# A hybrid transformer block on one core: four groups of w_down by seven products, a ring of four places, a new order of jobs

## The chip, the core and the metric

The kernel runs on one core of a Trainium2 chip. TensorE (PE) multiplies matrices, VectorE (DVE) and ScalarE (ACT) work on elements, GpSimd (POOL) here starts only DMAs that add to what they find, SyncE (SP) starts the other DMAs. The metric is the device time of one execution in microseconds (us); the profile is one further execution of the same program.

## What is computed

Two layers over x of 512 tokens by 1024 columns. Each layer norms x, projects it, runs three mixers side by side (a gated linear recurrence, a differential attention, a second recurrence), adds their projection to x, and ends in an MLP with a squared relu. The MLP is all that the change touches:

```
for l in range(DEPTH):                       # 2 layers
    ...                                      # mixers; x = x + mix @ w_out[l]
    h2 = rmsnorm(x, norm2_g[l])
    a = jnp.square(jax.nn.relu(h2 @ w_up[l]))      # 1024 -> 4096
    x = x + a @ w_down[l]                          # 4096 -> 1024
```

## The kernel before

A factor of a matrix product stands as two parts, a rounded high one (hi) and the rest (lo), and a product takes three matmuls, hi by hi, hi by lo and lo by hi. A weight **panel** of 512 KB is loaded, then made into `whi` and `wlo` in two halves: for each half ACT casts the raw data to `whi` (`halves`, L245) and DVE subtracts that from the raw data for `wlo` (L246). `whi` and `wlo` have three buffers each, so the casts of the panel of job n can start when the matmuls of job n-3 are done.

The 4096 columns between w_up and w_down are cut into 8 **groups** of 512, and the work on them into jobs, each of one panel:

- a **u** is one of seven products by which w_up of the next group is computed (`up_group`; seven products of quarter blocks in place of eight). In the order of the jobs they are p5, p1, p2, p7, p6, p4, p3; each has 24 matmuls of 128x256 (L1147 to L1149, in `product`). The results meet in `tmp` on DVE: after p6 three adds read the banks of p7 and p5 (L1183 to L1186), and p3 ends in L1197. `put` then takes relu and square on ACT and splits the result into hi and lo (`split`: cast L1090, subtraction L1091).
- a **d** is a quarter of an ordinary w_down group (`down_group`): 24 matmuls of 128x512 (L297 to L299), added to x by DVE (L1004).
- an **s** is one of seven products of a w_down group that is listed in `SEVEN`, here groups 2, 4 and 6 (`down_seven`): 12 matmuls of 128x512. It needs sums of quarter blocks of the squares (the **forms**), which DVE makes and `split` stores in the places `S["ah"][0]` and `S["al"][0]`, and its results go to x or to four accumulators (L1233, L1235, L1237), which `add_up` adds to x behind the last such group (L1258, L1262, L1267).

Some panels are sums of blocks of weights. They stand in four raw buffers (`raw(0)` to `raw(3)`, halves of the tiles mA and kT): SP loads a first block (`block_panel`, L262), and POOL starts a DMA that adds the next one to it (L264). The same buffer is then used by a later product: DMAs of POOL add a further block to it, once the halves of the product before have been read. So there are **chains**: in a u group p7 adds to what p1 used, p6 to what p5 used, and p3 to what p6 used. Panels that are no sums come through a ring of two buffers, `wraw`.

What sets the order is the table `ORDER`: string g gives the jobs of row g, which are the w_down of group g and the w_up of group g+1. The program is written out job by job, and the panel of job n+2 is begun ahead of job n (`AHEAD = 2`). Each engine then runs its instructions in its own order and waits for what is not yet there. In PSUM the results of p5, p7 and p3 share two banks (`ax`), p1 and p6 have one (`hx`), p2 and p4 one (`pv`), and the d and s jobs four (`mm`).

Of the kernel before, what the change touches and what calls it, by code (L numbers as in the profile page):

```python
# [15 lines left out]
P = 128  # L16
# [13 lines left out]
WP = 1056  # L30
WARM = 2
TOP = 1 << 24
SEVEN = (2, 4, 6)
ORDER = ("duduuduuduu", "uuduudududu", "usuusuusuus", "ususududusudud", "usuusuusuus", "ususududusudud", "usuusuusuus",
         "sssdddd")
RB = 3
COLS = dict(mq=0, mk=256, mv=512, mo=768, aq=1032, ak=1544, av=2056, hq=2568, hf=2824, hi=3080)

# [26 lines left out]
def hybrid_kernel(ctx, tc, x, norm1_g, w_in, conv_w, gate_b, mlstm_g, qn_g, kn_g, lam_v, subln_g,  # L65
# [16 lines left out]
    V = nc.vector  # L82
# [672 lines left out]
    steps = []  # L755

    def add_layer(l):
# [370 lines left out]
        def up_group(g):  # L1130


            c0 = g * 512
            w = {(i, j): w_up[l, (j - 1) * 512:j * 512, c0 + (i - 1) * 256:c0 + i * 256]
                 for i in (1, 2) for j in (1, 2)}
            st = {}
            tmp = [slab(13 + n // 2, 512, off=512 * (n % 2)) for n in range(4)]

            def product(wt, name, tag):
                pt = ps(tag)  # L1140
                wh, wl = wt
                hh, hl = S["F"][name]
                for c in range(2):
                    col = slice(c * P, (c + 1) * P)
                    dst = pt[:, c * 256:(c + 1) * 256]
                    for k in range(4):
                        mm(dst, wh[:, k, col], hh[:, k], start=k == 0, stop=False)  # L1147
                        mm(dst, wh[:, k, col], hl[:, k], start=False, stop=False)  # L1148
                        mm(dst, wl[:, k, col], hh[:, k], start=False, stop=k == 3)  # L1149
                return pt  # L1150

            def put(src, i, j):

                n = 2 * i + j
                tok = slice(j * 256, (j + 1) * 256)

                def two(v):
                    return v.rearrange("p (c t) -> p c t", c=2)
                r = slab(0, 512, off=512 * (n % 2))
                act(r, src, AF.Relu)  # L1160
                if g in SEVEN:
                    act(a4()[:, n], r, AF.Square)
                    if n in (0, 2):
                        split(*place(n // 2), a4()[:, n])
                else:
                    act(r, r, AF.Square)
                    split(S["ah"][1][:, 2 * i:2 * i + 2, tok], S["al"][1][:, 2 * i:2 * i + 2, tok], two(r))

            def p1(wt):
                nc.scalar.copy(tmp[0], product(wt, "b11", "hx"))  # L1170

            def p5(wt):
                st["5"] = product(wt, "t1", "ax")

            def p2(wt):
                V.tensor_add(tmp[3], product(wt, "b21", "pv"), tmp[0])
                put(tmp[3], 0, 0)

            def p7(wt):
                st["7"] = product(wt, "t3", "ax")  # L1180

            def p6(wt):
                V.tensor_sub(tmp[1], product(wt, "t2", "hx"), tmp[0])  # L1183
                V.tensor_add(tmp[2], st["7"], tmp[1])
                V.tensor_sub(tmp[0], tmp[2], st["5"])
                V.tensor_sub(tmp[3], st["5"], tmp[1])  # L1186
                put(tmp[0], 1, 1)

            def p4(wt):
                if g == 4 and l + 1 < DEPTH:  # L1190
                    load_gains(l + 1)
                    prms[l + 1] = load_params(l + 1)()
                V.tensor_add(tmp[2], product(wt, "t4", "pv"), tmp[2])
                put(tmp[2], 1, 0)

            def p3(wt):
                V.tensor_add(tmp[3], product(wt, "b22", "ax"), tmp[3])  # L1197
                put(tmp[3], 0, 1)
                if g in SEVEN:
                    a = a4()  # L1200
                    V.tensor_sub(a[:, 0], a[:, 0], a[:, 1])
                    split(*place(2), a[:, 0])
                    V.tensor_sub(a[:, 1], a[:, 1], a[:, 3])
                    split(*place(3), a[:, 1])

            one, two_ = (0, 1) if g % 2 else (1, 0)
            return [((lambda: block_panel(raw(two_), w[2, 1], [w[2, 2]])), p5),
                    ((lambda: block_panel(raw(one), w[1, 1], [])), p1),
                    ((lambda: block_panel(in_ring(), w[1, 2], [])), p2),
                    ((lambda: block_panel(raw(one), None, [w[2, 1]])), p7),  # L1210
                    ((lambda: block_panel(raw(two_), None, [w[1, 1]])), p6),
                    ((lambda: block_panel(in_ring(), w[2, 2], [])), p4),
                    ((lambda: block_panel(raw(two_), None, [w[1, 2]])), p3)]

        def down_seven(g):

            w = {(i, j): w_down[l, g * 512 + (j - 1) * 256:g * 512 + j * 256, (i - 1) * 512:i * 512]
                 for i in (1, 2) for j in (1, 2)}  # L1220

            def product(wt, n, to, after=None):
                hi, lo = (t.rearrange("p (k t) -> p k t", k=2) for t in place(n))
                for c in range(2):
                    pt = ps("mm")
                    tok = slice(c * P, (c + 1) * P)
                    nat_mm(pt, 512, lambda k: hi[:, k, tok], lambda k: lo[:, k, tok], *wt,
                           [(0, 0), (1, 1)], True, True)
                    with tc.high_priority():
                        if isinstance(to, tuple):  # L1230
                            i, j = to
                            d = xs[2 * j + c][:, i * 512:(i + 1) * 512]
                            V.tensor_add(d, d, pt)  # L1233
                        elif g == SEVEN[0]:
                            nc.scalar.copy(acc(to)[:, c], pt)  # L1235
                        else:
                            V.tensor_add(acc(to)[:, c], acc(to)[:, c], pt)  # L1237
                if after:
                    after()

            def t2():
                a = a4()
                V.tensor_add(a[:, 0], a[:, 0], a[:, 3])
                split(*place(0), a[:, 0])

            def t4():
                a = a4()
                V.tensor_sub(a[:, 0], a[:, 2], a[:, 0])
                split(*place(1), a[:, 0])

            def b22():
                split(*place(2), a4()[:, 3])

            def add_up():
                def to_x(i, j, op, n):
                    for c in range(2):
                        d = xs[2 * j + c][:, i * 512:(i + 1) * 512]
                        op(d, d, acc(n)[:, c])  # L1258

                def s0():  # L1260
                    to_x(0, 0, V.tensor_add, 0)
                    V.tensor_sub(acc(2), acc(2), acc(0))  # L1262
                    to_x(0, 1, V.tensor_add, 1)
                    to_x(0, 1, V.tensor_sub, 2)

                def s1():
                    V.tensor_add(acc(3), acc(3), acc(2))  # L1267
                    to_x(1, 0, V.tensor_add, 3)
                    to_x(1, 1, V.tensor_add, 3)
                    to_x(1, 1, V.tensor_sub, 1)  # L1270
                if g == SEVEN[-1]:
                    steps.extend([s0, s1])

            def pan(r, fresh, add):
                return lambda: block_panel(r(), fresh, add, 512)
            one, two = (lambda: raw(2)), (lambda: raw(3))
            return [(pan(one, w[1, 1], []), None, None, lambda t: product(t, 0, 0)),
                    (pan(in_ring, w[1, 2], []), None, None, lambda t: product(t, 1, (0, 0), t2)),
                    (pan(two, w[2, 1], [w[2, 2]]), None, None, lambda t: product(t, 2, 1, t4)),
                    (pan(one, None, [w[2, 1]]), None, None, lambda t: product(t, 3, 3, b22)),  # L1280
                    (pan(two, None, [w[1, 1]]), None, None, lambda t: product(t, 0, 2)),
                    (pan(in_ring, w[2, 2], []), None, None, lambda t: product(t, 1, (1, 0))),
                    (pan(two, None, [w[1, 2]]), None, None, lambda t: product(t, 2, (0, 1), add_up))]

        def down_group(g):
            def st(i):
                return tuple((lambda k, t=t[g % 2]: t[:, k, i * P:(i + 1) * P]) for t in (S["ah"], S["al"]))

            def done(i, cols):
                if g < NG - 1:  # L1290
# [75 lines left out]
```

## Time and profile before

| | |
|---|---|
| median of 3 runs | 1270.45 us (1269.99 to 1270.73) |
| the profiled execution, device time | 1270.51 us |
| its span | 1268.7 us |
| PE busy | 1255.0 us, 99% |
| DVE busy | 987.2 us, 78% |
| ACT busy | 748.4 us, 59% |
| POOL busy | 120.5 us, 9% |
| MLP rows 0 to 7, layer 0 | 326.7 to 641 us |
| MLP rows 0 to 7, layer 1 | 956 to 1268 us |

Times inside the profile count from the start of the span; some 1.8 us of the execution lie outside it. A busy engine is one that has an instruction under way, and matmuls overlap, so the distance from start to start says what a matmul costs, not the time of one. The granted clock (PEclk, 1.00 is full) is TensorE's alone.

### The profile page before, as it was taken

The numbers are of one execution on the slowest core, as the hardware profiler recorded it, in microseconds if no ns is written. First come the engines' busy times: TensorE is split into PE (matmuls) and PEld (weight loads), VectorE is DVE, ScalarE is ACT, GpSimd is POOL, SyncE is SP. The second block draws the span as 40 slices with busy tenths as digits, with TensorE's granted clock in tenths as the row PEclk, the third lists the DMA queues.
The fourth block names the chain that finished last, engine by engine and source line by source line (L and its number), as shares of the span: only waits on it lengthen the run. The fifth ranks groups of instructions, "written<-read, shape, count | busy, mean of one in ns | idle before, by whom it ended". The sixth has DMA issues, their size and how long they took to land.

```text
span 1268.7 us, 20162 instructions
## 1 busy us (share of the span) xinstructions
PE 1255.0 (99%) x7420; PEld 1076.1 (85%) x7420; DVE 987.2 (78%) x2190; ACT 748.4 (59%) x1607; POOL 120.5 (9%) x116
## 2 busy tenths in 40 slices
PE   9999999999999999999999999999999999999998
PEld 6788777888999988989787887788888989899896
DVE  6786887988966868779967767879888677677787
ACT  6754785638644745545556457756386547456461
POOL 0000000000011211211000000000001112121210
PEclk9999999999999999999999999999999999999999
DMA  7322211216576987877433222112265779878863
GB/s 212 84 67 70 66 34 51 83 55 170 130 166 133 197 188 164 183 183 134 116 83 83 68 74 61 34 50 83 64 170 117 167 143 198 195 155 203 171 123 110
DMA packets 116758, 153.43 MB, mean 121 GB/s; under 512 B 5738, under 2 KB 80052, under 8 KB 116660
## 3 DMA queue, kind: packets, MB, share of 16 engines
q1 hardware_dynamic: 80228, 109.66, 27.9%
q0 software_dynamic: 36096, 41.95, 21.6%
q8 instruction: 58, 0.95, 0.3%
q10 hardware_dynamic: 336, 0.54, 0.1%
q14 instruction: 40, 0.33, 0.1%
HBM read 150.03 MB, written 2.10 MB: 120 GB/s over the span
## 4 chain that ended last, share of the span: by engine, by line
PE 83%; DVE 6%; ACT 5%; DMA 3%; issue 1%; SPq 0%; POOL 0%; ACTq 0%; DVEq 0%; POOLq 0%
PE pmm L299 14%; PE pmm L297 14%; PE pmm L298 14%; PE pmm L305 3%; PE pmm L306 3%; PE pmm L304 3%; PE pax L1148 3%; PE pax L1147 3%; PE pax L1149 3%; PE pax L687 2%; PE phx L1148 2%; PE phx L1149 2%; PE phx L1147 2%; PE ppv L1147 2%; PE ppv L1148 2%; PE ppv L1149 2%
## 5 line engine op out<-in xcount | busy, mean ns | idle before, releaser
L297 PE MATMUL pmm<-whi,h 128*128 128x512 f32 (+2 forms) x484 | 187.3, 387 | 0.1
L298 PE MATMUL pmm<-wlo,h 128*128 128x512 f32 (+2 forms) x484 | 185.5, 384 | 0.2 <-DVE wlo L246 0.2
L245 ACT CAST whi<-wraw 128x512 fp32r<-128x512 f32 x192 | 109.4, 618 | 123.9 <-PE pmm L299 64.1
L299 PE MATMUL pmm<-whi,h 128*128 128x512 f32 (+2 forms) x452 | 173.3, 383 | 0.1
L246 DVE TENSOR_TENSOR wlo<-wraw,whi 128x512 fp32r<-128x512 f32 x192 | 125.7, 687 | 45.5 <-ACT whi L245 45.4
L288 ACT ACTIVATE whi<-wraw,gcol 128x256 fp32r<-128x256 f32 (+2 forms) x192 | 99.5, 572 | 80.3 <-PE pmm L299 63.9
L289 DVE SCALAR_TENSOR_TENSOR wlo<-wraw,gcol,whi 128x256 fp32r<-128x256 f32 (+2 forms) x192 | 101.8, 569 | 43.2 <-ACT whi L288 40.8
L298 PEld LDWEIGHTS pmm<-wlo,h 128*128 128x128 f32 x484 | 91.1, 188 | 16.9 <-DVE wlo L246 1.0
L297 PEld LDWEIGHTS pmm<-whi,h 128*128 128x128 f32 x484 | 91.1, 188 | 16.1 <-ACT h L343 0.5
L297 PE MATMUL pmm<-whi,yb 128*128 128x512 f32 (+2 forms) x256 | 100.4, 392 | 0.0
L299 PEld LDWEIGHTS pmm<-whi,h 128*128 128x128 f32 x452 | 85.0, 188 | 16.2 <-DVE h L1091 0.6
L298 PE MATMUL pmm<-wlo,yb 128*128 128x512 f32 (+2 forms) x256 | 98.5, 385 | 0.0
L245 ACT CAST whi<-kT 128x512 fp32r<-128x512 f32 x108 | 61.6, 618 | 52.5 <-DMA kT<-in_w_up_dram 14.1
L298 PE MATMUL pmm<-wlo,ya 128*128 128x512 f32 (+2 forms) x228 | 87.3, 383 | 0.0
L297 PE MATMUL pmm<-whi,ya 128*128 128x512 f32 (+2 forms) x228 | 87.3, 383 | 0.0
L299 PE MATMUL pmm<-whi,yd 128*128 128x512 f32 (+2 forms) x224 | 86.3, 385 | 0.3 <-DVE yd L1091 0.3
L246 DVE TENSOR_TENSOR wlo<-kT,whi 128x512 fp32r<-128x512 f32 x108 | 69.6, 685 | 19.0 <-ACT whi L245 18.4
L1004 DVE TENSOR_TENSOR x<-x,pmm 128x512 f32<-128x512 f32 x96 | 65.5, 683 | 22.4 <-PE pmm L299 21.4
L245 ACT CAST whi<-mA 128x512 fp32r<-128x512 f32 x92 | 52.4, 617 | 48.9 <-PE pmm L299 21.5
L299 PE MATMUL pmm<-whi,yc 128*128 128x512 f32 (+2 forms) x212 | 80.9, 381 | 0.0
L264 POOL DMA_DIRECT2D kT<-in_w_up_dram x30 | 38.9, 1298 | 409.9 <-DVE wlo L246 248.2
L246 DVE TENSOR_TENSOR wlo<-mA,whi 128x512 fp32r<-128x512 f32 x92 | 59.3, 685 | 13.6 <-ACT whi L245 13.6
(479 smaller groups left out, 3526.9 us busy)
## 6 DMA issues: line engine op xcount, KB each, us to landing
wraw<-in_w_down_dram SPq DMA_DIRECT2D x52, 512.0 KB
wraw<-in_w_in_dram SPq DMA_DIRECT2D x51, 512.0 KB
wraw<-in_w_up_dram SPq DMA_DIRECT2D x36, 512.0 KB
kT<-in_w_up_dram POOLq DMA_DIRECT2D x30, 512.0 KB, 6.5
mA<-in_w_up_dram POOLq DMA_DIRECT2D x26, 512.0 KB, 6.8
kT<-in_w_down_dram POOLq DMA_DIRECT2D x18, 512.0 KB, 7.3
wraw<-in_w_out_dram SPq DMA_DIRECT2D x16, 512.0 KB
mA<-in_w_up_dram SPq DMA_DIRECT2D x14, 512.0 KB
```

Of the source, the lines that this page charges most:

```text
L245: nc.scalar.copy(hi[:, ch], raw[:, ch])
L246: V.tensor_sub(lo[:, ch], raw[:, ch], hi[:, ch].bitcast(F32))
L264: nc.gpsimd.dma_start(out=v3(raw), in_=rows(b), accum_op=ALU.add)
L288: act(hi[:, ch], raw[:, ch], AF.Copy, scale=g)
L289: V.scalar_tensor_tensor(lo[:, ch], raw[:, ch], g, hi[:, ch].bitcast(F32), op0=ALU.mult, op1=ALU.subtract)
L297: mm(pt[:, :n], sh(a), wh[:, b], start=first and j == 0, stop=False)
L298: mm(pt[:, :n], sh(a), wl[:, b], start=False, stop=False)
L299: mm(pt[:, :n], sl(a), wh[:, b], start=False, stop=last and j == nk - 1)
L1004: V.tensor_add(xs[i][:, cols], xs[i][:, cols], pt)
L1147: mm(dst, wh[:, k, col], hh[:, k], start=k == 0, stop=False)
L1148: mm(dst, wh[:, k, col], hl[:, k], start=False, stop=False)
L1149: mm(dst, wl[:, k, col], hh[:, k], start=False, stop=k == 3)
```

## The change

Groups 2, 3, 4 and 5 are computed by seven products, not 2, 4 and 6. So two such groups follow each other, and the forms of group g+1 take places that products of group g still read: a small table says what each form needs (`needs`), `happened` is called behind each square and each product, and makes each form as soon as all it needs has happened, in a ring of four places. `BUF` says in which of the two buffers an ordinary group's squares stand: group 1 in buffer 1 as before, from which its jobs now run as late as row 4, group 6 in buffer 1 and group 7 in buffer 0. `add_up` follows group 5. `ORDER` is rewritten.

```diff
-SEVEN = (2, 4, 6)
-ORDER = ("duduuduuduu", "uuduudududu", "usuusuusuus", "ususududusudud", "usuusuusuus", "ususududusudud", "usuusuusuus",
-         "sssdddd")
+SEVEN = (2, 3, 4, 5)
+ORDER = ("duduuduuduu", "uuuuuuu", "susususdudsususu", "sususususususu", "susususdudsususu", "suusuusuusu",
+         "sususuduuduudd", "dddd")
...
+        BUF = {g: g % 2 for g in range(NG)}
+        BUF.update({NG - 2: 1, NG - 1: 0})
...
+        def form(g, k):
+            a = a4()
+            if k == 2:
+                V.tensor_sub(a[:, 0], a[:, 0], a[:, 1])
+            elif k == 3:
+                V.tensor_sub(a[:, 1], a[:, 1], a[:, 3])
+            elif k == 4:
+                V.tensor_add(a[:, 0], a[:, 0], a[:, 3])
+            elif k == 5:
+                V.tensor_sub(a[:, 0], a[:, 2], a[:, 0])
+            split(*place(k % 4), a[:, (0, 2, 0, 1, 0, 0, 3)[k]])
...
+        def happened(*what):
+            kind, g, n = what
...
+            seen.add(what)
+            for f in [f for f in forms]:
+                if needs(*f) <= seen:
+                    form(*f)
+                    forms.remove(f)
+                    seen.add(("form",) + f)
...
                 if g in SEVEN:
                     act(a4()[:, n], r, AF.Square)
-                    if n in (0, 2):
-                        split(*place(n // 2), a4()[:, n])
+                    happened("put", g, n)
                 else:
                     act(r, r, AF.Square)
-                    split(S["ah"][1][:, 2 * i:2 * i + 2, tok], S["al"][1][:, 2 * i:2 * i + 2, tok], two(r))
+                    ah, al = S["ah"][BUF[g]], S["al"][BUF[g]]
+                    split(ah[:, 2 * i:2 * i + 2, tok], al[:, 2 * i:2 * i + 2, tok], two(r))
...
-            def product(wt, n, to, after=None):
-                hi, lo = (t.rearrange("p (k t) -> p k t", k=2) for t in place(n))
+            def product(wt, n, to):
+                assert ("form", g, n) in seen
+                hi, lo = (t.rearrange("p (k t) -> p k t", k=2) for t in place(n % 4))
...
+                happened("product", g, n)
+                if n == 6 and g == SEVEN[-1]:
+                    add_up()
...
-                return tuple((lambda k, t=t[g % 2]: t[:, k, i * P:(i + 1) * P]) for t in (S["ah"], S["al"]))
+                return tuple((lambda k, t=t[BUF[g]]: t[:, k, i * P:(i + 1) * P]) for t in (S["ah"], S["al"]))
```

What this moves on the engines is seen in row 1, where the products of w_up of group 2 stand. The lines of the changed kernel have other numbers: L1176 is L1219 there, L1183 to L1186 are L1226 to L1229, L1160 is L1203, L1162 and L1166 are L1205 and L1208, L1170 is L1213.

DVE in layer 0, before, from the panel of p4 to that of p3. In a row the line stands first, then the operation, and what is written and read; wlo_587 is the low half of p4's panel, wlo_591 that of the fourth quarter of group 1, wlo_597 that of p3; phx_588 is the bank of p6's result, pax_581 that of p7, pax_564 that of p5:

```order
L246 TENSOR_TENSOR wlo_587_4020<-wraw_585_4018,whi_586_4019 128x512 x2
L1183 TENSOR_TENSOR big_67<-phx_588_4026,big_67 128x512
L246 TENSOR_TENSOR wlo_591_4059<-wraw_589_4057,whi_590_4058 128x512 x2
L1184 TENSOR_TENSOR big_67<-pax_581_3957,big_67 128x512
L1185 TENSOR_TENSOR big_67<-big_67,pax_564_3818 128x512
L1186 TENSOR_TENSOR big_67<-pax_564_3818,big_67 128x512
L246 TENSOR_TENSOR wlo_597_4094<-mA_523_3435,whi_596_4093 128x512 x2
```

Here p6's add (L1183) and the three adds that read the banks of p7 and p5 (L1184 to L1186) stand ahead of the halves of p3's panel.

DVE in layer 0 now, from the panel of p7 (wlo_566) on; wlo_569 is the low half of p6's panel, wlo_573 of p4's, wlo_576 of p3's, wlo_579 of the first product of group 2's w_down; phx_577 is the bank of p6's result, pax_574 that of p7:

```order
L246 TENSOR_TENSOR wlo_566_3844<-kT_511_3316,whi_565_3843 128x512 x2
L1091 TENSOR_TENSOR h3_502_3192<-big_67,h1_500_3190 128x2x256
L246 TENSOR_TENSOR wlo_569_3877<-mA_523_3435,whi_568_3876 128x512 x2
L1219 TENSOR_TENSOR big_67<-ppv_570_3883,big_67 128x512
L246 TENSOR_TENSOR wlo_573_3915<-wraw_571_3913,whi_572_3914 128x512 x2
L1091 TENSOR_TENSOR h2_501_3191<-big_67,h0_499_3189 128x512
L246 TENSOR_TENSOR wlo_576_3947<-mA_523_3435,whi_575_3946 128x512 x2
L1226 TENSOR_TENSOR big_67<-phx_577_3953,big_67 128x512
L246 TENSOR_TENSOR wlo_579_3985<-mA_523_3435,whi_578_3984 128x512 x2
L1227 TENSOR_TENSOR big_67<-pax_574_3921,big_67 128x512
```

The halves of p3's panel and those of the product after it now stand ahead of L1227, the add that reads p7's bank. On PE the first matmul of p3 (L1190, pax_583, p3's bank) waits for this L1227.

ACT in layer 0, before, from the casts of p2's panel (whi_566) to those of p6's (whi_579); whi_569 is p7's, whi_576 that of the second quarter of group 1:

```order
L245 CAST whi_566_3844<-wraw_565_3843 128x512 x2
L1166 ACTIVATE big_67<-big_67 128x512
L1090 CAST h1_500_3190<-big_67 128x2x256
L245 CAST whi_569_3877<-kT_511_3316 128x512 x2
L1170 COPY big_67<-phx_568_3851 128x512
L245 CAST whi_576_3913<-wraw_575_3912 128x512 x2
L245 CAST whi_579_3950<-mA_523_3435 128x512 x2
```

ACT in layer 0 now, from the casts of p7's panel (whi_565) to those of p3's (whi_575); whi_568 is p6's, whi_572 p4's:

```order
L245 CAST whi_565_3843<-kT_511_3316 128x512 x2
L1208 ACTIVATE big_67<-big_67 128x512
L1090 CAST h1_500_3190<-big_67 128x2x256
L245 CAST whi_568_3876<-mA_523_3435 128x512 x2
L1213 COPY big_67<-phx_567_3850 128x512
L245 CAST whi_572_3914<-wraw_571_3913 128x512 x2
L1203 ACTIVATE big_67<-big_67 128x512
L1205 ACTIVATE big_67<-big_67 128x512
L1090 CAST h0_499_3189<-big_67 128x512
L245 CAST whi_575_3946<-mA_523_3435 128x512 x2
```

The square and the cast of the group before (L1208 and L1090; before L1166 and L1090) now stand behind the casts of p7's panel, and ahead of those of p6's panel; no panel of group 1 stands between p7's and p6's, nor between p6's and p3's.

## Rows read from the trace of the kernel before

**Rows 1.** The page, part 1: busy us (share of the span) x instructions, by engine.

```profile
PE 1255.0 (99%) x7420; PEld 1076.1 (85%) x7420; DVE 987.2 (78%) x2190; ACT 748.4 (59%) x1607; POOL 120.5 (9%) x116
```

**Rows 2.** Busy time by stretch: us, PE, PEld, DVE, ACT, POOL busy (x), PEclk, DMA share, GB/s.

```profile
575.00:605.90 30.90, 30.90 (x218) 28.80 (x217) 28.55 (x47) 19.50 (x36) 5.00 (x4) 1.00 0.63 122
605.90:641.00 35.10, 34.14 (x161) 27.20 (x160) 32.46 (x58) 18.54 (x43) 1.79 (x3) 1.00 0.41 116
...
430.00:440.00 10.00, 10.00 (x72) 9.30 (x71) 8.79 (x15) 8.23 (x16) 1.04 (x1) 1.00 1.11 260
```

**Rows 3.** Timeline of PE: start us, us, engine line op out<-in [idle before <-releaser].

```profile
371.62 0.28 PE L1147 MATMUL phx<-mid,whi 128*128 128x256 f32 x1
...
374.45 0.39 PE L297 MATMUL pmm<-whi,h 128*128 128x512 f32 x1
...
380.00 0.28 PE L1147 MATMUL ppv<-ya,whi 128*128 128x256 f32 x1
...
1000.75 0.28 PE L1147 MATMUL phx<-mid,whi 128*128 128x256 f32 x1
```

**Rows 4.** Timeline of PE, at the places where its starts lie apart.

```profile
537.88 0.40 PE L297 MATMUL pmm<-whi,h 128*128 128x512 f32 x1
...
539.49 0.50 PE L298 MATMUL pmm<-wlo,h 128*128 128x512 f32 x1 [0.23 <-DVE wlo L246]
...
617.18 0.40 PE L298 MATMUL pmm<-wlo,h 128*128 128x512 f32 x1
617.72 0.50 PE L299 MATMUL pmm<-whi,h 128*128 128x512 f32 x1
...
622.90 0.40 PE L297 MATMUL pmm<-whi,h 128*128 128x512 f32 x1
624.10 0.66 PE L340 MATMUL pax<-cst,x 128*128 128x128 f32 x4 [0.81 <-DVE x L1004]
...
1244.62 0.39 PE L298 MATMUL pmm<-wlo,yb 128*128 128x512 f32 x1
1245.32 0.50 PE L299 MATMUL pmm<-whi,yd 128*128 128x512 f32 x1 [0.30 <-DVE yd L1091]
```

**Rows 5.** Timeline of ACT, DVE and POOL, layer 0, around the landing of a summed panel.

```profile
368.34 1.28 POOL L264 DMA_DIRECT2D kT<-in_w_up_dram  x1 [1.41 <-DVE wlo L246]
...
373.16 0.63 ACT L1166 ACTIVATE big<-big 128x512 f32<-128x512 f32 x1
373.81 0.62 ACT L1090 CAST h<-big 128x512 fp32r<-128x512 f32 x1
374.93 1.14 ACT L245 CAST whi<-kT 128x512 fp32r<-128x512 f32 x2 [0.50 <-DMA kT<-in_w_up_dram]
...
366.76 1.28 DVE L246 TENSOR_TENSOR wlo<-kT,whi 128x512 fp32r<-128x512 f32 x2
...
375.59 1.29 DVE L246 TENSOR_TENSOR wlo<-kT,whi 128x512 fp32r<-128x512 f32 x2 [0.43 <-ACT whi L245]
```

**Rows 6.** The same of layer 1: POOL, ACT, DVE.

```profile
997.58 1.28 POOL L264 DMA_DIRECT2D kT<-in_w_up_dram  x1 [1.48 <-DVE wlo L246]
...
1004.46 1.14 ACT L245 CAST whi<-kT 128x512 fp32r<-128x512 f32 x2 [0.79 <-DMA kT<-in_w_up_dram]
...
1005.12 1.29 DVE L246 TENSOR_TENSOR wlo<-kT,whi 128x512 fp32r<-128x512 f32 x2 [0.72 <-ACT whi L245]
```

**Rows 7.** Landings: the chain of waits, 1226 to 1240; issues of 360 to 400.

```profile
1230.39 5.83 DMA kT<-in_w_down_dram
...
kT<-in_w_up_dram POOLq DMA_DIRECT2D x2, 512.0 KB, 7.3
```

**Rows 8.** The end of the span: last matmul of the timeline; windows with the granted clock.

```profile
1264.31 0.40 PE L299 MATMUL pmm<-whi,yd 128*128 128x512 f32 x1
...
1268.00:1268.80 0.80, 0.00 (x0) 0.00 (x0) 0.00 (x0) 0.00 (x0) 0.00 (x0) 0.99 0.00 0
1268.80:1269.50 0.70, 0.00 (x0) 0.00 (x0) 0.00 (x0) 0.00 (x0) 0.00 (x0) 0.50 0.00 0
```

More of the change, by code (lines that the diff above doesn't have):

```diff
@@ L1119, in place, with needs @@
             return S["ah"][0][:, n], S["al"][0][:, n]
+        seen = set()
+        forms = []
+        def form(g, k):
[9 more added lines that the diff above has]
+            split(*place(k % 4), a[:, (0, 2, 0, 1, 0, 0, 3)[k]])
+        def needs(g, k):
+            of = (("put", 0),), (("put", 2),), (("form", 0), ("put", 1)), (("form", 2), ("put", 3)), \
+                (("form", 2), ("put", 3)), (("form", 4), ("form", 1)), (("put", 3),)
+            r = {(w, g, n) for w, n in of[k]}
+            if k >= 4:
+                r.add(("product", g, k - 4))
+            elif g - 1 in SEVEN:
+                r.add(("product", g - 1, (4, 5, 6, 3)[k]))
+            return r
+        def happened(*what):
+            kind, g, n = what
+            if kind == "put":
+                assert g - 1 not in SEVEN or {("form", g - 1, k) for k in ((5,), (3,), (5,), (3, 4, 6))[n]} <= seen
+                if n == 0:
+                    forms.extend((g, k) for k in range(7))
+            seen.add(what)
[4 more added lines that the diff above has]
+                    seen.add(("form",) + f)
         def acc(n):
@@ L1198, in p3 @@
                 put(tmp[3], 0, 1)
[L1199 to L1204, printed above, removed]
             one, two_ = (0, 1) if g % 2 else (1, 0)
@@ L1237, in product @@
                             V.tensor_add(acc(to)[:, c], acc(to)[:, c], pt)
[L1238 to L1252, printed above, removed]
+                happened("product", g, n)
+                if n == 6 and g == SEVEN[-1]:
+                    add_up()
             def add_up():
@@ L1270, in s1 @@
                     to_x(1, 1, V.tensor_sub, 1)
-                if g == SEVEN[-1]:
-                    steps.extend([s0, s1])
+                steps.extend([s0, s1])
             def pan(r, fresh, add):
@@ L1276, in down_seven @@
             one, two = (lambda: raw(2)), (lambda: raw(3))
[L1277 to L1283, printed above, removed]
+            pans = (pan(one, w[1, 1], []), pan(in_ring, w[1, 2], []), pan(two, w[2, 1], [w[2, 2]]),
+                    pan(one, None, [w[2, 1]]), pan(two, None, [w[1, 1]]), pan(in_ring, w[2, 2], []),
+                    pan(two, None, [w[1, 2]]))
+            to = (0, (0, 0), 1, 3, 2, (1, 0), (0, 1))
+            return [(p, None, None, lambda t, n=n: product(t, n, to[n])) for n, p in enumerate(pans)]
         def down_group(g):
             def st(i):
-                return tuple((lambda k, t=t[g % 2]: t[:, k, i * P:(i + 1) * P]) for t in (S["ah"], S["al"]))
+                return tuple((lambda k, t=t[BUF[g]]: t[:, k, i * P:(i + 1) * P]) for t in (S["ah"], S["al"]))
             def done(i, cols):
```

## The prediction

> **What bounds the kernel now.** I read the page's first part before anything else: PE is busy for 99% of the span and DVE for 78% [rows 1]. So time goes only where PE's matmuls grow fewer, or where PE stands still. The table of windows, cut at the rows of the MLP, says the same of each row: in row 6 of layer 0 PE is busy for 30.90 of 30.90 us, in row 7 for 34.14 of 35.10, and DVE for 92% of both [rows 2]. The timeline of PE then gives the price of a job by start-to-start distance, since matmuls overlap: the 24 matmuls of a u take 374.45 - 371.62 = 2.83 us, the 24 of 128x512 of a d take 380.00 - 374.45 = 5.55 [rows 3]; an s has 12 of those, 2.78. Last I looked for places where starts lie further apart [rows 4]. With PE full, the prediction is: fewer matmuls, minus old stalls, plus new ones. The profiled execution took 1270.51 us (span 1268.7 and 1.8 around it), 0.06 above the median of 1270.45, so the sum on it stands for the median too.
>
> **Fewer matmuls: -5.6.** One group more by seven products has 7 s of 12 matmuls, 84, in place of 4 d of 24, 96. That is 12 fewer per layer and 24 in all, and PE's list in the order of the two programs is shorter by 24. At 5.55 / 24 = 0.231 us each [rows 3] they are worth 5.55 us.
>
> The Trainium skill, page TensorE: Matmul & The Clock Gate, section Back-to-back issue gap, gives about 131 ns for a sustained matmul of 512 columns. By it the term would be 24 x 0.131 = 3.1 us; the row's 0.231 is of this very instruction form, and the measurement decides.
>
> **Old stalls that go: -2.4.** Four places of before [rows 4]. At 537.88 to 539.49 four distances take 1.61 instead of 0.93: a ring panel is late (+0.68). At 617.18 to 617.72 +0.31, and at 622.90 to 624.10, +0.97, DVE is held by `add_up`, which in before comes in the full row 7; in layer 1 at 1244.62 to 1245.32, +0.47. Together 2.43. In the new order `add_up` comes behind group 5, and row 7 is four d alone, with 22 us of PE work for the DVE ops of four panels. What is late next there I find nowhere in the order, so I take it all, between 1.5 (the add_up ones return in row 5 in part) and 2.4.
>
> **The new wait in row 1: +10.0.** Row 1 is now seven u in a row. p7, p6 and p3 stand in chains: POOL adds a block to a raw buffer only when the halves of the panel before in that buffer have been read. In before, 13.9 us of matmuls (two d and p4: 5.55 + 2.83 + 5.55) lay between the end of p6 and the start of p3; now only p4's 2.83. I follow it in layer 0; the order up to p2 is unchanged, so the times of before hold to there.
> - p7's halves: POOL issues at 368.34, 0.30 behind the end of the subtractions that it waits for (366.76 + 1.28); its data is there at 374.93, 6.59 later; the subtractions end at 375.59 + 1.29 = 376.88 [rows 5].
> - p6's halves: on ACT the square and the cast of the group before, done at 374.43 in before, now stand behind p7's casts [rows 5], 0.63 + 0.62 more, and then p6's casts. From p7's casts to p6's that is 1.05 + 1.25 = 2.3, so p6's subtractions end at 379.2. Its data has long landed.
> - p3's block: issue 0.30 later at 379.5, landing 6.6 later at 386.1. p3 would start, five u behind p1's first matmul at 371.62 [rows 3], at 385.77, so the panel itself is about on time; what is late is another thing.
> - PE's first matmul of p3 waits, in the program, for L1227 on DVE, the add that reads p7's bank, and ahead of it DVE now has p3's own two halves, L1226, and the two halves of the next product. DVE takes 28.55 / 47 = 0.607 us for an operation in a full row [rows 2]. From the landing to L1227's end it is 0.66 (cast to subtraction, 374.93 to 375.59 [rows 5]), five more operations of 0.607 and the 0.68 that the last one takes, 4.37. So L1227 ends at 390.44, and PE waits 4.67 us.
> - Layer 1: issue 997.58, data 1004.46, 6.88 later, subtractions to 1006.41 [rows 6]; with 2.3 + 0.30 + 6.88 the block is there at 1015.89, and 4.37 later, at 1020.26, L1227 has ended, against 1000.75 + 5 x 2.83 = 1014.90 [rows 3]: 5.36 us, 10.03 in the two layers.
>
> The landing of p3's block is the unknown. From below 5.83 us, the shortest in the chain of waits [rows 7], which takes 0.76 + 1.05 = 1.8 off; from above, two POOL loads of 360 to 400 have a median of 7.3 [rows 7], and as one took 6.6 the other took 8.0, which adds 1.4 + 1.1 = 2.5. I take 6.6 and 6.88, those of the same buffers at this very place. So 8.2 to 12.5 for the two.
>
> Behind L1227 on DVE stand the adds L1228 and L1229 and the split of p6's result, which nobody needs before group 2's second form. ACT's squares wait with them; the next products that need them come behind p3 and the first s, 5.6 us later.
>
> **The clock: +2.0.** In the rows PE's last matmul ends at 1264.71, the granted clock is 0.99 in the window to 1268.80 and 0.50 behind it, the lower of its two levels [rows 8], so the fall came 4.1 us behind the last matmul. The idle of 0.81 us at 624.10 [rows 4] was not followed by a fall. The two new waits leave PE idle for about 4.6 and 5.2. How long the lower level would then last no row shows; as an estimate, as long as the 4.1 us from the last matmul to the fall, half of them lost: 2.0 a fall. I take one fall in the two waits, between none (0) and two (4.1).
>
> **Nothing for the rest.** SP's list is as long as before. POOL starts 8 accumulating DMAs more; in the rows with s four jobs or more, 11.3 us, lie between the links of a chain, where a landing takes 6 to 8. DVE has 38 instructions more in all, six subtractions, three splits, four form adds and six adds of accumulators per layer among them. In row 3, u4 with s3, 14 jobs bring 60 DVE operations, 60 x 0.607 = 36.4 of 14 x 2.83 = 39.6 us, 92%, what row 6 of before had without a stall [rows 2]; if that cover is gone, it is the fourth rival. ACT, busy for 59% of the span [rows 1], has eighteen instructions more in all. Loads: 16 of 0.52 MB in those 39.6 us are 212 GB/s, and 10 us of before moved 260 with PE full [rows 2].
>
> **Sum.** 1270.51 - 5.55 - 2.43 + 10.0 + 2.0 = 1274.5 us. My measure of no change is 0.2%, 2.5 us, about what a measurement of this kernel can tell: 1267.9 to 1273.0.
>
> **Rivals.**
> 1. The clock holds in both waits, since each is hardly longer than the idle in which it fell. For it: one fall in the whole trace, and that behind the last matmul. Then 1272.5, no change. It decides only if the waits are as computed or shorter, up to 10.5 in all; above that the time is slower without the clock.
> 2. The clock falls in both: 1276.5. For it: in both PE would be idle for longer than ahead of the one fall that the rows show. This is also what the Trainium skill, page TensorE: Matmul & The Clock Gate, section HAM oscillation, makes of it: matmuls that wait for a transfer start again at half rate, each time. No row here shows more than the one fall at the end.
> 3. PE waits for p3's panel and not for L1227: the place is the bank that p3 gets, the price the low half alone, which the third matmul needs, 2 x 0.118 behind the first: 386.07 + 0.66 + 0.68 - 0.24 = 387.17 in layer 0 and 1016.99 in layer 1, so 1.4 and 2.1 us of wait, no fall: 1270.5 - 8.0 + 3.5 = 1266.0, faster. It decides from a total wait below 5.5 us. Against it: the wait for L1227 stands in PE's list.
> 4. DVE doesn't keep pace in the long rows with s, at 92%. Row 7 of before, at the same 92%, lost 0.96 of 35.1 us [rows 2]; at that rate the 21 jobs of 59.4 us lose 1.6 per layer, 3.2 in all: 1277.7. Against it: row 6 lost nothing.
>
> That the change doesn't do what it says is out: the 24 matmuls are counted in the order, and so is the position of L1227.
>
> **How the numbers follow.** Forecast with one fall 0.42, first rival 0.20, second 0.15, third 0.10, fourth 0.13. Of the forecast's share 0.04 has landings so short (-1.8) that it ends at 1272.7. Faster is the third, 0.10; no change the first and that 0.04, 0.24; slower the rest, 0.66. The range reaches from the first rival with short landings of p7's and p3's blocks (1272.5 - 3.6 = 1268.9) to the second with long ones (1276.5 + 2.5 = 1279.0), and leaves out the third.
>
> **What would show it.** In the changed trace p3's first matmul of group 2 should stand idle before 390 and before 1020, 4 to 6 us each, released by DVE's L1227, with the raw data at some 386 and 1016; the granted clock should show one dip there, of some 4 us; the stalls of [rows 4] should be gone, and PE's starts in rows 2 to 5 be 0.118 and 0.231 apart throughout. If the wait is under 2 us, the step on L1227 is wrong; if PE has gaps before L245's or L246's panels in rows 2 to 5, the step on DVE is.

## The result, and the profile after

The changed kernel takes 1289.74 us (median of 4, 1289.51 to 1290.0), the kernel before beside it 1270.59: 1.0147 times as long, 95% interval 1.0134 to 1.0159. It is slower, as forecast, but by 19 us, where I had said 4, and far above the range of 1269 to 1279. The profiled execution took 1290.0 us, its span is 1288.2, 19.5 more than before. The page of the changed kernel, its first line and the first part, as in [rows 1]:

```profile
span 1288.2 us, 20185 instructions
...
PE 1259.9 (98%) x7396; PEld 1080.8 (84%) x7396; DVE 1006.7 (78%) x2228; ACT 756.9 (59%) x1625; POOL 129.9 (10%) x124
```

PE is still the engine that is always busy (98%), and yet it has 24 matmuls fewer. So I looked for the places where it stands still. The timeline of PE (columns as in [rows 3]) has four long ones, two in each layer:

```profile
391.82 0.36 PE L1190 MATMUL pax<-yd,whi 128*128 128x256 f32 x1 [4.25 <-DVE big L1227]
...
569.04 0.35 PE L1190 MATMUL pax<-yd,whi 128*128 128x256 f32 x1 [3.11 <-DVE big L1227]
...
1028.67 0.55 PE L1190 MATMUL pax<-h,whi 128*128 128x256 f32 x1 [4.99 <-DVE big L1227]
...
1206.89 0.35 PE L1190 MATMUL pax<-h,whi 128*128 128x256 f32 x1 [3.83 <-DVE big L1227]
```

Each is the first matmul of a p3, and each waits for L1227 on DVE. The first and the third are p3 of group 2 in row 1, which the prediction had. The second and the fourth are p3 of group 6 in row 5, which it had not. The windows of the same trace (columns as in [rows 2]; the granted clock is the third value from the end) show what comes behind the first:

```profile
385.00:390.00 5.00, 2.57 (x22) 2.36 (x20) 2.02 (x4) 2.17 (x4) 0.00 (x0) 1.00 1.10 223
390.00:395.00 5.00, 3.18 (x16) 3.21 (x17) 4.76 (x8) 2.31 (x4) 1.69 (x2) 0.71 0.93 187
395.00:400.00 5.00, 5.00 (x31) 4.50 (x31) 1.89 (x3) 3.65 (x8) 0.80 (x1) 0.94 1.08 171
```

Half the clock for 0.29 x 2 of five us and 0.06 x 2 of the next five is 3.5 us at the lower level. It is as long behind the second (0.96 and 0.70 from 565 to 575) and the fourth (0.79 and 0.87 from 1205 to 1215), and twice as long, 6.8 us, at the third, where it begins before p3 starts:

```profile
1023.00:1028.00 5.00, 0.69 (x7) 0.49 (x5) 3.17 (x6) 2.18 (x4) 0.00 (x0) 0.90 1.11 224
1028.00:1033.00 5.00, 4.33 (x20) 4.36 (x21) 3.62 (x6) 2.30 (x4) 2.50 (x2) 0.50 0.90 203
1033.00:1038.00 5.00, 5.00 (x30) 4.46 (x28) 1.89 (x3) 4.04 (x8) 0.00 (x0) 0.92 0.98 156
```

So the clock fell four times, once at every wait.

The difference of the two spans, put together from the starts on PE:

| | forecast | trace |
|---|---|---|
| 24 matmuls fewer | -5.55 | -5.55 |
| stalls of [rows 4] | -2.43 | -2.4, all gone |
| waits of row 1, two layers | +10.03 | 4.42 + 5.14 = +9.6 |
| waits of row 5, two layers | 0 | 3.28 + 4.00 = +7.3 |
| lower clock in the MLP | +2.0, one fall | +7.3, four falls |
| before the MLP, at the start | 0 | +1.6 |
| new stalls of 0.66 (the gains of layer 1, at 483.6) and 0.35 | 0 | +1.0 |
| sum | +4.0 | +18.8 of 19.5 |

A wait is the distance of two starts less what it is elsewhere (0.118 or 0.232). The lower clock is the excess of 77 distances of about 0.21 and 0.43 us in the MLP rows, against 2 in the kernel before. The 0.7 that are left I have not assigned. The 1.6 at the start have nothing to do with the change, since the two programs are the same there: the first matmuls of 512 columns came 0.43 apart until 13.05 us, in the kernel before 0.23 from 9.72 on; of the fourteen profiles of this study, three have their two hundredth matmul at 49.3 to 49.5 us, the others at 47.6 to 48.5. In these three the trace's first record of the granted clock stands at 13.3 us, in the others at 4.5 to 7.6; ahead of that record the windows print 1.00, which is no reading.

### The profile page after: what moved, and what is told of

The parts are those of the page before. It is cut to its first block, busy times and chain, and to the rows that moved or that the text cites. A ratio compares the mean times of both kernels' runs of the same rounds, so it can differ in the third digit from the quotient of the medians.

```text
span 1288.2 us, 20185 instructions
## 1 busy us (share of the span) xinstructions
PE 1259.9 (98%) x7396; PEld 1080.8 (84%) x7396; DVE 1006.7 (78%) x2228; ACT 756.9 (59%) x1625; POOL 129.9 (10%) x124
## 4 chain that ended last, share of the span: by engine, by line
PE 77%; DMA 8%; DVE 7%; ACT 4%; issue 2%; POOL 1%; SPq 0%; POOLq 0%; ACTq 0%; DVEq 0%
PE pmm L297 14%; PE pmm L299 14%; PE pmm L298 14%; DMA mA<-in_w_up_dram 4%; PE pmm L306 3%; PE pmm L305 3%; PE pmm L304 3%; PE pax L687 3%; DMA kT<-in_w_up_dram 2%; PE pax L1190 2%; PE pax L1192 2%; PE pax L1191 2%; DVE wlo L246 2%; PE ppv L708 2%; PE phx L1191 1%
## 5 line engine op out<-in xcount | busy, mean ns | idle before, releaser
L245 ACT CAST whi<-wraw 128x512 fp32r<-128x512 f32 x184 | 105.1, 618 | 102.0 <-PE pmm L299 73.9
L246 DVE TENSOR_TENSOR wlo<-wraw,whi 128x512 fp32r<-128x512 f32 x184 | 120.0, 686 | 26.4 <-ACT whi L245 26.0
L298 PE MATMUL pmm<-wlo,ya 128*128 128x512 f32 (+2 forms) x288 | 111.1, 386 | 0.0
L297 PE MATMUL pmm<-whi,ya 128*128 128x512 f32 (+2 forms) x288 | 111.1, 386 | 0.0
L245 ACT CAST whi<-kT 128x512 fp32r<-128x512 f32 x120 | 68.5, 618 | 67.4 <-PE pmm L299 14.7
L299 PE MATMUL pmm<-whi,yc 128*128 128x512 f32 (+2 forms) x272 | 104.7, 385 | 0.2 <-DVE yc L1091 0.2
L246 DVE TENSOR_TENSOR wlo<-kT,whi 128x512 fp32r<-128x512 f32 x120 | 77.4, 684 | 30.0 <-ACT whi L245 29.8
L245 ACT CAST whi<-mA 128x512 fp32r<-128x512 f32 x100 | 56.7, 618 | 59.5 <-DMA mA<-in_w_up_dram 26.1
L246 DVE TENSOR_TENSOR wlo<-mA,whi 128x512 fp32r<-128x512 f32 x100 | 64.8, 684 | 26.6 <-ACT whi L245 26.3
L1004 DVE TENSOR_TENSOR x<-x,pmm 128x512 f32<-128x512 f32 x80 | 54.7, 684 | 27.0 <-PE pmm L299 26.5
L297 PE MATMUL pmm<-whi,yb 128*128 128x512 f32 (+2 forms) x192 | 75.1, 391 | 0.0
L298 PE MATMUL pmm<-wlo,yb 128*128 128x512 f32 (+2 forms) x192 | 73.3, 382 | 0.0
L1191 PE MATMUL phx<-mid,whi 128*128 128x256 f32 x224 | 63.0, 281 | 0.0
L1190 PE MATMUL phx<-mid,whi 128*128 128x256 f32 x224 | 63.0, 281 | 0.0
```

Source lines behind the costliest of these rows:

```text
L245: nc.scalar.copy(hi[:, ch], raw[:, ch])
L246: V.tensor_sub(lo[:, ch], raw[:, ch], hi[:, ch].bitcast(F32))
L297: mm(pt[:, :n], sh(a), wh[:, b], start=first and j == 0, stop=False)
L298: mm(pt[:, :n], sh(a), wl[:, b], start=False, stop=False)
L299: mm(pt[:, :n], sl(a), wh[:, b], start=False, stop=last and j == nk - 1)
L1004: V.tensor_add(xs[i][:, cols], xs[i][:, cols], pt)
```

## Experiments

Four things could make the 19 us: the short chain in row 1, something in row 5, the bank that p3 waits for, and the clock. In the kernels below, line numbers stand one lower where `ORDER` takes one line less (L1226 for L1227, L245 for L246). The kernel before, run beside each batch, had medians of 1270.59 to 1272.01 us, so a difference of one us between batches says little.

**The clock by itself (e4_warm).** Matmuls that nobody reads are put ahead of p3, which waits anyway:

```diff
             def p3(wt):
+                if g in (2, 6):
+                    pt = ps("mm")
+                    hh = S["F"]["b11"][0]
+                    for k in range(36 if g == 2 else 26):
+                        mm(pt[:, 0:256], hh[:, 0, 0:P], hh[:, 1], start=True, stop=True)
```

> The changed kernel with matmuls of no use, 128x256, ahead of p3 in groups 2 (36 of them, 4.2 us) and 6 (26, 3.1 us), which nobody reads: they fill most of the waits and lengthen none. Theory of the clock: no fall in the four waits, and the 2.0 us of each are saved: 1281.7 us. Rival, the low clock is hidden by other waits behind it: 1289.7 or more.

Measured: 1283.34 us, 6.4 less than the changed kernel. The timeline of PE and the windows around the wait of row 1 in layer 0:

```profile
386.22 1.00 PE L1244 MATMUL pmm<-mid 128*128 128x256 f32 x7
...
390.00:395.00 5.00, 5.00 (x38) 4.70 (x38) 3.25 (x6) 3.93 (x7) 2.35 (x2) 1.00 0.91 193
395.00:400.00 5.00, 5.00 (x35) 4.60 (x34) 4.16 (x7) 4.68 (x10) 0.00 (x0) 1.00 0.91 148
```

The 36 matmuls fill the time in which PE stood still, and the clock stays at 1.00, here and in the windows of the other three waits. So the lower clock did cost about what the distances gave, 7.3 us or 1.8 a fall on average. The 6.4 of the medians are a net figure: in the profile the four p3 also start 2.0 us less late, since the matmuls put in last 14.9 us where PE had waited 16.8, and some 2 us of other small waits came. Work of no use made the changed kernel faster, though not faster than the one before.

**The bank (e3_bank).** p3 of groups 2 and 6 takes one of the four banks:

```diff
-                V.tensor_add(tmp[3], product(wt, "b22", "ax"), tmp[3])
+                V.tensor_add(tmp[3], product(wt, "b22", "mm" if g in (2, 6) else "ax"), tmp[3])
```

> The changed kernel in which the product p3 of groups 2 and 6 takes a bank of the four (mm) in place of one of the two (ax), so that its first matmul doesn't wait for the add that reads p7's bank. Theory of the bank: the four waits shrink to what the panel itself needs, about 1.0, 1.7, 1.8 and 2.4, 6.9 in place of 16.8, too short for a fall of the clock: 1289.7 - 9.9 - 8.0 = 1271.8 us. If the clock falls all the same, 1279.8. Rival, the panel alone decides: 1289.7.

Measured: 1281.14 us, 8.6 less, and 9 short of what I expected. The timeline of PE, where it stands still in row 2 of layer 0 and in row 5 of both layers, and the chain of waits (start us, us, what) ahead of the last:

```profile
397.65 0.50 PE L297 MATMUL pmm<-whi,h 128*128 128x512 f32 x1 [2.23 <-ACT h L1090]
...
564.85 0.38 PE L1190 MATMUL pmm<-yd,whi 128*128 128x256 f32 x1 [1.30 <-ACT whi L245]
...
1196.91 0.45 PE L1190 MATMUL pmm<-h,whi 128*128 128x256 f32 x1 [2.20 <-ACT whi L245]
...
1182.77 2.41 DMA kT<-in_w_down_dram
1185.18 10.96 DMA mA<-in_w_up_dram
```

The wait for L1227 is gone, and p3 in row 1 of layer 0 waits 0.35 us for its panel. But a part comes back further on: a product of group 2 waits 2.2 us for a split on ACT (L1090), whose data comes from p4's add (L1236), which stands on DVE behind the same adds; the same came back in layer 1 (2.4 us by the starts). And in row 5 of layer 1 the panel itself is late: its adding DMA took 10.96 us. Behind the first and the last of these three rows the clock fell (0.84 and 0.82 in the windows from 395 to 405, 0.81 and 0.85 from 1194 to 1204). So the bank is one of two links in row 1. In row 5 the bank and the panel share the wait: without the bank's part p3 still waits 1.5 and 2.4 us there for its panel, in place of 3.3 and 4.0.

**Row 5 in the old pattern (e2_row5).**

```diff
- "suusuusuusu"        # row 5
+ "usuusuusuus"
```

> The changed kernel with row 5 in the pattern of the rows before (usuusuusuus for suusuusuusu). Theory: the place of the s against the u in row 5 brings POOL's adding DMAs together, so that they land 8 to 10 us after their issue; in the old pattern they land in 6 to 7 and the waits of row 5 (3.3 and 4.0) go with two falls of the clock: 1289.7 - 7.3 - 4.0 = 1278.4 us. Rival, the chain from p6 to p3 is too short there as in row 1, whatever the pattern (two jobs lie between in both): 1289.7, no change.

Measured: 1294.50 us, 4.8 more. The pattern is not it: PE's wait before p3 grew to 6.9 us in layer 0. (About 1 of the 4.8 is in the waits of row 1, 5.0 and 5.8 here, which this edit does not touch.)

POOL's adding DMAs just ahead of it, in its timeline:

```profile
556.11 1.28 POOL L263 DMA_DIRECT2D kT<-in_w_up_dram  x1 [14.71 <-DVE x L1270]
556.87 1.85 POOL L263 DMA_DIRECT2D mA<-in_w_up_dram  x1
557.62 2.33 POOL L263 DMA_DIRECT2D kT<-in_w_down_dram  x1
```

Three within 1.5 us; p3's, the second, landed 9.8 us after its issue, the third after 12.5. The changed kernel has the same burst, and there p3's is the last. Its POOL rows, and p3's landing in the chain of waits, in layer 0 and layer 1:

```profile
553.72 1.19 POOL L264 DMA_DIRECT2D kT<-in_w_down_dram  x1 [12.24 <-DVE wlo L246]
555.50 1.33 POOL L264 DMA_DIRECT2D kT<-in_w_up_dram  x1 [0.59 <-issue]
556.29 1.87 POOL L264 DMA_DIRECT2D mA<-in_w_up_dram  x1
...
540.19 8.20 DMA kT<-in_w_up_dram
...
556.29 9.96 DMA mA<-in_w_up_dram
...
1193.52 10.57 DMA mA<-in_w_up_dram
```

The view of DMA issues from 553 to 557 gives the landings of the first two (the last value, us from the issue):

```profile
kT<-in_w_down_dram POOLq DMA_DIRECT2D x1, 512.0 KB, 5.9
kT<-in_w_up_dram POOLq DMA_DIRECT2D x1, 512.0 KB, 6.9
```

The three landings are at 559.6, 562.4 and 566.2: one behind the other, 2.8 and 3.8 us apart, though they were issued within 2.6.

**One DMA of the burst less (e7_noadd).**

```diff
-            return [((lambda: block_panel(raw(two_), w[2, 1], [w[2, 2]])), p5),
+            return [((lambda: block_panel(raw(two_), w[2, 1], [] if g == 7 else [w[2, 2]])), p5),
```

> The changed kernel in which the first panel of w_up of group 7 (p5) leaves out its second block, so that one adding DMA of 512 KB less is in the burst of row 5, ahead of that of p3; all engines but POOL do the same work. Theory of POOL's queue: p3's block lands in 7 us in place of 10, the two waits of row 5 shrink to 0.4 each, without a fall: 1289.7 - 6.5 - 4.0 = 1279.2 us. Rival, DVE's backlog sets the wait: unchanged, 1289.7.

Measured: 1280.79 us, 8.9 less (10.5 expected). POOL's timeline, and the landing in the chain of waits:

```profile
553.69 1.19 POOL L264 DMA_DIRECT2D kT<-in_w_down_dram  x1 [12.22 <-DVE wlo L246]
556.51 1.33 POOL L264 DMA_DIRECT2D mA<-in_w_up_dram  x1 [1.63 <-DVE wlo L246]
...
556.51 6.91 DMA mA<-in_w_up_dram
```

Issued at nearly the same time, p3's block now lands after 6.91 us, and PE waits 0.45 us in place of 3.28 (layer 1: 0.49 in place of 4.00), with no fall of the clock in row 5. No engine but POOL has less to do, so what was late in row 5 was the burst on POOL's queue, not DVE's work.

**p3 later (e5_late6).** The same cause, attacked from the other side: the burst stays, but p3 comes two jobs later.

```diff
- "suusuusuusu", "sususuduuduudd",      # rows 5 and 6
+ "suusuusuus", "ssuusuuduuduudd",
```

> The changed kernel with p3 of group 6 two jobs later (rows 5 and 6: suusuusuus, ssuusuuduuduudd), so that four jobs, 11 us, lie between p6 and p3 there. Theory of POOL's queue: the adding DMAs land one behind the other, 3 to 4 us apart, and p3's, third of a burst, takes 10 us; with 11 us of matmuls ahead of p3 that is hidden, the waits of row 5 (3.3 and 4.0) go with their two falls of the clock (2.0 each): 1289.7 - 7.3 - 4.0 = 1278.4 us. Rival, DVE is behind in rows 4 and 5 and any panel is late there: the wait moves to the next jobs, 1287 or more.

Measured: 1278.94 us, against 1278.4 expected. POOL still issues its three within 2.7 us, and p3's first matmul at 571.40 waits for nothing:

```profile
554.10 1.19 POOL L263 DMA_DIRECT2D kT<-in_w_down_dram  x1 [13.23 <-DVE wlo L245]
555.97 1.33 POOL L263 DMA_DIRECT2D kT<-in_w_up_dram  x1 [0.69 <-DMA kT<-in_w_up_dram]
556.76 1.87 POOL L263 DMA_DIRECT2D mA<-in_w_up_dram  x1
...
571.40 0.28 PE L1189 MATMUL pax<-yd,whi 128*128 128x256 f32 x1
```

**Row 1 as before (e1_row1), and with two d (e8_two).**

```diff
- "uuuuuuu", "susususdudsususu", "sususususususu", "susususdudsususu",      # rows 1 to 4
+ "uuduudududu", "sususususususu", "sususususususu", "sususususususu",      # e1_row1
+ "uuuuududu", "sususususususu", "sususususususu", "susususdudsususu",      # e8_two
```

> The changed kernel with row 1 as it was before (uuduudududu) and the four jobs d of group 1 taken out of rows 2 and 4. Theory of spacing: p3's wait of row 1 (4.4 us in layer 0, 5.1 in layer 1) goes, and with each its fall of the clock (2.0), so 1289.7 - 9.5 - 4.0 = 1276.2 us; the waits of row 5 (3.3 and 4.0) stay. Rival, the jobs d in rows 2 and 4 are what gives DVE room there: then new gaps of PE stand in rows 2 to 4, and the time stays over 1282.

> The changed kernel with row 1 as uuuuududu and row 2 without d, rows 4 to 6 as they are: the same as e6_both without the later p3. Theory: the waits of row 1 and their falls go, those of row 5 stay: 1289.7 - 9.5 - 4.0 = 1276.2 us. Rival, as in e1_row1 the loss comes back in rows 2 to 5: 1285 or more.

Measured: 1288.41 and 1285.40 us. 1276.2 had been expected of both. The waits of row 1 are gone, as expected, and yet most of the time stays. In e1_row1 PE stands still at two other places of layer 0, and the second has the old cause (timeline of PE; chain of waits):

```profile
490.74 0.24 PE L178 MATMUL phx<-cst,r 25*128 25x25 f32 x1 [2.88 <-DVE gcol L238]
...
569.59 0.35 PE L1189 MATMUL pax<-yd,whi 128*128 128x256 f32 x1 [3.92 <-DVE big L1226]
...
556.60 10.20 DMA mA<-in_w_up_dram
```

The first is a small transposition in p4 of group 4, in row 3, where the gains of layer 1 are loaded: PE waits for DVE to copy them (L238), and DVE's copy stands in its queue behind the halves of panels. In the changed kernel that cost 0.66 us; with the d gone from row 2, 3.0 in layer 0, with a fall of the clock behind it. In layer 1, which has no next layer's gains to load, rows 2 and 3 of e1_row1 show no such gap. e8_two has the same stall (2.8 us, at 476.5) and both waits of row 5. So the d in row 2 did do something: they left room ahead of that copy.

In layer 1 both lose time at one more product, behind which the clock fell too: e1_row1 at p7 of row 5, e8_two at p3 of row 3 (timeline of PE; chain of waits):

```profile
1183.29 0.38 PE L1189 MATMUL pax<-h,whi 128*128 128x256 f32 x1 [1.49 <-ACT whi L244]
...
1173.09 9.45 DMA kT<-in_w_up_dram
```

```profile
1113.51 0.39 PE L1189 MATMUL pax<-h,whi 128*128 128x256 f32 x1 [1.45 <-ACT whi L244]
...
1100.84 11.90 DMA mA<-in_w_up_dram
```

Both blocks are the third of three under way. So late landings are not a matter of row 5 alone: in row 3 three jobs, 8.4 us, lie between p6 and p3, and that was not enough for 11.9.

**Both places (e6_both).** e8_two with the later p3.

> As e5_late6, and two of group 1's jobs d in row 1 (uuuuududu), none in row 2, two in row 4 as in the changed kernel. If spacing in both places is all that costs: 1289.7 - 9.5 - 7.3 - 8.0 = 1264.9 us, 0.4% below the kernel before. Rival, the d of row 2 are wanted there by DVE and POOL: gaps in rows 2 to 5 and over 1275.

Measured: 1270.15 us beside 1271.69 of the kernel before, ratio 0.9984, interval 0.9967 to 1.0000. The waits for p3 in rows 1 and 5 are gone; one of 0.6 us is left in row 3 of layer 1, whose block landed after 11.58. What the profiled run lacks to 1264.9 stands mainly in the first of these rows of the timeline of PE, with a fall of the clock behind it (0.50 in the window from 479 to 485); the second row is that p3:

```profile
479.47 0.29 PE L178 MATMUL phx<-cst,r 25*128 25x25 f32 x1 [2.90 <-DVE gcol L238]
...
1107.92 0.39 PE L1189 MATMUL pax<-h,whi 128*128 128x256 f32 x1 [0.46 <-ACT whi L244]
```

Of its ten runs, from 1264.41 to 1273.65 us, the fastest is the one whose mean granted clock was 1.000.

**The gains elsewhere (e9_gains, e11_g7, e12_g1).** e6_both with one number changed, 2, 7 and 1 in place of 4:

```diff
-                if g == 4 and l + 1 < DEPTH:
+                if g == 2 and l + 1 < DEPTH:        # e9_gains; 7 in e11_g7, 1 in e12_g1
```

> As e6_both, with the loading of the next layer's gains and parameters in p4 of group 2 (row 1) in place of group 4 (row 3). In e6_both PE stood still for 3.1 us in row 3 of layer 0 until DVE had copied the gains, and the clock fell behind it (3.0 us at the lower level more than elsewhere). Theory: row 1 has room on DVE, so both go: 1270.2 - 3.1 - 3.0 = 1264.1 us, 0.5% below the kernel before. Rival, the copy is late in row 1 just as well, behind the halves of the panels there: 1270, as e6_both.

> As e9_gains, with the loading of the gains in p4 of group 7 (row 6). In e9_gains PE still stood for 2.4 us in row 1, since DVE's copy of the gains stood behind the halves of a panel that had not landed and the adds behind them. Row 6 has d jobs of 5.6 us around it, and DVE is 64% busy from 611 to 645 us: the wait goes, 1269.9 - 2.4 = 1267.5 us, and some runs lose a fall of the clock less. Rival, the copy stands behind late halves there too: 1270.

> As e9_gains, with the loading of the gains in p4 of group 1 (row 0, whose order no version here touches). DVE is 80% busy there and no panel was late: 1269.9 - 2.4 = 1267.5 us. Rival, the copy stands behind halves of a panel that is not yet there, as in row 1: 1270.

Measured: 1269.89, 1268.59 and 1265.92 us, ratios to the kernel before of 0.9982 (0.9973 to 0.9991), 0.9972 (0.9961 to 0.9983) and 0.9953 (0.9938 to 0.9968). In e9_gains the copy is late again, now behind halves that wait for a panel of the ring to land (timeline of PE and of DVE):

```profile
391.29 0.24 PE L178 MATMUL phx<-cst,r 25*128 25x25 f32 x1 [2.27 <-DVE gcol L238]
...
387.93 1.29 DVE L245 TENSOR_TENSOR wlo<-wraw,whi 128x512 fp32r<-128x512 f32 x2 [4.04 <-ACT whi L244]
389.14 0.68 DVE L1226 TENSOR_TENSOR big<-pax,big 128x512 f32<-128x512 f32 x1
389.86 0.69 DVE L1227 TENSOR_TENSOR big<-big,pax 128x512 f32<-128x512 f32 x1
390.46 0.68 DVE L1228 TENSOR_TENSOR big<-pax,big 128x512 f32<-128x512 f32 x1
391.06 0.17 DVE L238 COPY gcol<-phx 128x16 f32<-128x16 f32 x1
```

In row 6 it still costs 1.5 us, in row 0 nothing. All three intervals lie below 1; e12_g1 is the fastest, 5.7 us below the kernel before and 24 below the changed one. Its page:

```profile
span 1264.8 us, 20185 instructions
...
PE 1252.0 (99%) x7396; PEld 1073.2 (85%) x7396; DVE 1005.4 (79%) x2228; ACT 757.1 (60%) x1625; POOL 129.9 (10%) x124
```

**The two d of row 4 in row 2 (e10_early).**

> As e9_gains, with the two d of row 4 in row 2. What is told apart is where DVE is behind: if in rows 2 and 3, the gaps of e6_both in layer 1 (0.6 and two of 0.4 at 1107 to 1117) go and the time is some 1.4 us under e9_gains, 1262.7; if in rows 4 and 5, new gaps stand there and the time is 2 us or more above e9_gains.

Measured: 1273.53 us, 3.6 more than e9_gains. The gaps of layer 1 in row 3 (0.6 and 0.4) went, and others of up to 2.6 us came in row 5; the longest is p7's, whose block landed 10.6 us after its issue. So the d of row 4 are worth more there than in row 2: without them panels are late in row 5.

## Why the prediction was wrong, point by point

**Fewer matmuls, old stalls.** Right: PE has 24 matmuls fewer, and none of the four old stalls is left.

**The wait of row 1.** Right in mechanism and size: the block for p3 was issued at 380.85, landed 6.40 us later and L1227 ended at 391.68, where I had 379.5, 6.6 and 390.44 on a time base that started 1.6 earlier. 4.42 and 5.14 us were lost for 4.67 and 5.36. PE's releaser is L1227 in all four, so the third rival is out. e3_bank adds what I had left out: behind L1227 stand more things than I said that "nobody needs"; without the bank's wait 2.4 us came back at the second s.

**Nothing for the rest.** This is the step that failed. It said that in the rows with s "four jobs or more, 11.3 us, lie between the links of a chain, where a landing takes 6 to 8". Both halves are wrong for row 5. There, in suusuusuusu, p6 and p3 have p4 and one s between them, 5.6 us, half of what I said (in row 1 it is p4's 2.83). Rows 2 to 4 have three jobs there, 8.4 us, and not four either. And a landing takes 10 in row 5. I had bounded it at 8.0 by two issues of 360 to 400, where POOL had little to do. The kernel before has the longer ones too, in row 4, and they could have been read. The view of DMA issues of 506 to 511 (the last value is the time to landing in us), in the order of their issue:

```profile
kT<-in_w_up_dram POOLq DMA_DIRECT2D x1, 512.0 KB, 6.3
mA<-in_w_up_dram POOLq DMA_DIRECT2D x1, 512.0 KB, 8.4
kT<-in_w_down_dram POOLq DMA_DIRECT2D x1, 512.0 KB, 9.7
```

Three issued within 3.3 us. That cost the kernel before nothing in row 4, with the same two jobs between p6 and p3 (usuusuusuus), because p3's block was the first of the three. In row 5 of the changed kernel it is the third: the s of group 5 and the first product of group 7 are ahead of it. e7_noadd and e5_late6 show it from both sides. What the late block then cost, 7.3 us with two falls of the clock on top, went through L1227 as in row 1; e3_bank has 3.8 without that.

The Trainium skill, page DMA: Bandwidth & Descriptors, section Anatomy of one DMA — SWDGE (gpsimd) path, fits a DMA from POOL by 2.0 us and its bytes at 436 KB per us, for 512 KB an estimate of 3.2 us. The shortest adding DMA of the changed kernel's MLP took 5.7 from issue to landing, so the fit is low for this kind.

**The clock.** This term, too, was too small, 2.0 for 7.3. A fall cost 1.8 us on average (some 1.6 where the lower level lasted 3.5 us, 2.3 where it lasted 6.8), where I had estimated 2.0; but it fell at all four waits, not at one in two, and two of them I did not have. The two falls of row 1 alone are the second rival, which I gave 0.15, and should have been the forecast: both idle stretches, 4.4 and 5.1, were longer than the 4.1 that the rows showed before a fall. The waits of 3.3 and 4.0 were followed by one too, one of 3.1 in e6_both, two of 2.4 in e3_bank, and those of 1.7 and 1.6 in layer 1 of e1_row1 and e8_two. One of 2.4 in e9_gains was not, nor the third of 2.4 in e3_bank, nor 2.5 and 2.6 in e10_early, nor 3.5 in e8_two (p3 of row 5 in layer 1), nor those of 0.5 in e7_noadd. So in these runs the waits longer than 3.5 us all came with a fall, and from 1.6 to 3.5 the length of the wait does not tell.

**The fourth rival, DVE at 92%.** It pointed to the rows with s, but the wrong cause, and its price of 3.2 us was less than half of what was lost there. DVE is busy for 92%, 85% and 83% of rows 3, 4 and 5 of the changed kernel in layer 0, and for 92%, 87% and 91% in e12_g1, where PE has no gap of 0.7 us or more between starts there. Where it shows is the copy of the gains: PE waits for a DVE operation of 0.17 us that stands behind halves in DVE's queue.

**The size of it.** My 4.0, the 7.3 of row 5, 5.3 more for the clock, 1.6 at the start and 1.0 of small stalls less 0.4 in row 1 are 18.8. The chances came from one place of the program that I had followed to the end; 0.13 for all that could happen in rows 2 to 6 was too little, since I had not followed their chains in the same way.

**What stays open.** Which of the s and u in row 5 of e10_early bring their blocks together was not followed further. Why the clock fell at some waits of 1.6 to 3.5 us and not at others, these runs do not show. That p7's block in row 5 was late too (8.2 us, issued at 540.19) and how much of the burst it made was not tried by itself.

## What to carry to other kernels

A chain in which each transfer waits until the data of the last has been read has a least spacing: list every pair of links in the new order, in matmul time between them, and set it against the landing of a transfer that is last in a burst, not of a lonely one. A landing time is a property of the queue at that moment, so take its bound from the busiest stretch of the trace. And when an idle stretch of TensorE is found, add the price of the clock behind it at once; here four falls added 7.3 us to 16.8 us of waits, the one in e6_both 2.7 to 3.1, and that was had back with matmuls of no use, with more work between the links, or by moving one small operation that PE waited for.

## What the runs showed of the hardware

Adding DMAs of 512 KB from POOL in the MLP, with no other of them under way, landed 5.8 to 6.9 us after their issue in the fourteen traces (once 7.7). When three were issued within 3.4 us they landed one behind the other, 2.6 to 6.1 us apart, and the third took 9.0 to 12.5 us. TensorE's clock fell to its lower level at every wait of more than 3.5 us in the MLP, at some from 1.6 to 3.5 and not at others; the lower level lasted 3.4 or 6.8 us, with matmuls near half their pace, 0.21 in place of 0.118 us from start to start, and a fall cost 1.5 to 2.7 us in the changed kernel and e6_both. At the start of the program matmuls came at half their pace until some 13 us in three of the fourteen profiles; the trace has no record of the granted clock until 13.3 us there, and what the windows print ahead of it, 1.00, is no reading.
